# One PSUM tile in place of four pools: denominators between numerators, three rotating halves at the start, paired banks in the drain, w and u loaded first

## The chip, the cores and the metric

The kernel runs on one core of one Trainium2 chip. The metric is device time in microseconds (us) of one execution. Engines are named as in the profile: PE (matmul), DVE (vector), ACT (activation), POOL (GpSimd), SP. Each engine runs its instructions in the order in which the program lists them and waits on semaphores for the others.

## The reference

For each of 16 batches and 256 channels it is a recurrence over 2048 steps (RWKV's "wkv"): a weighted mean of all v so far, the weights being exponentials that decay with w, with a bonus u for the current step.

```python
for t in range(seq_len):
    ww = u + k[b, t]
    qq = np.maximum(pp, ww)
    e1, e2 = np.exp(pp - qq), np.exp(ww - qq)
    output[b, t] = (e1 * aa + e2 * v[b, t]) / (e1 * bb + e2 + 1e-08)
    ww = pp - w + k[b, t]
    qq = np.maximum(ww, k[b, t])
    e1, e2 = np.exp(ww - qq), np.exp(k[b, t] - qq)
    aa, bb, pp = e1 * aa + e2 * v[b, t], e1 * bb + e2, qq
```

k and v are float32 [16, 2048, 256] (33.5 MB each), w and u are [256], and the output has the shape of v.

## The kernel before

The recurrence is cut into chunks of 128 time steps. The 128 partitions hold the 128 steps of a chunk, and a **tile** holds one chunk of four batches: 128 x 1024 values. There are 16 chunks of 4 tiles, so 64 tiles, numbered n = 4c + p. One tile is 512 KB of k, 512 KB of v and 512 KB of output.

A tile passes through these functions:

- `load`: two DMAs, k (tile `kr`) and v (tile `vr`; for every fourth tile from 9 on the DMA casts v itself to bf16, tile `vb`). Nearly all loads and all stores are issued by POOL, in program order, six tiles ahead (`AHEAD`).
- `round_k` (DVE): casts k to the matmul's float32 form, tile `km`, two buffers.
- `logs` (PE): four one- or two-row matmuls (L171) put in the terms of w and u, four full matmuls (L175) add a weighted k. Result: logarithms `X`, two kinds (decayed keys, and keys with the bonus) of two banks each, so four of PSUM's eight banks, one buffer.
- `exps` (ACT): one activation over all four banks, 2048 values a partition, into two planes of the ring `EZR` (12 tiles deep, bf16).
- `cast_v`, `times_v` (DVE): v to bf16, and its product with both planes into the ring's other two planes.
- `den` (PE): running sums along time by triangular matrices, 4 matmuls into `den` (two banks). `recip` (ACT): an Ln and an Exp of 1024 values each give the reciprocal `rd`.
- `num` (PE): the same for one half i of the numerator, 2 matmuls into `num` (one bank). `mult` (DVE): that half times `rd`, 512 values, into `ot`; then `store` (POOL).

Ten iterations (`LAG`) after its `exps`, a tile gets `den` and `recip`; one iteration later `num`, `mult` and `store`. The lag is there for the state that passes from chunk to chunk: some ten small instructions a chunk (`sums`, `copy_sums`, `turn`, `state_logs`, `state_offsets`, `state_weights`, `state_chain`, `turn_back`, `inject`) are spread by the table `later` over six iterations. Their PSUM scratch is the eighth bank (`misc`), and `inject` ends with four small DMAs on SP that write the state into the ring, where `den` and `num` of the next chunk read it.

One loop of 76 iterations does all this; every call is wrapped in `K(...)`, which keeps the written order on each engine. Iterations 0 to 10 write no output yet, and the last 12 (the **drain**) load and exponentiate nothing. In iteration n, `qp = n - 11` is the tile whose numerators are made and `q = n - 10` the tile of `recip`; `den` runs one iteration ahead (`q1`):

```python
num(qp, 0); exps(n); round_k(n + 2); mult(qp, 0); cast_v(n + 1)
num(qp, 1); mult(qp, 1); store(qp); times_v(n); logs(n + 1)
recip(q); den(q1)
```

Of the kernel before, what the change touches and what calls it, by code (L numbers as in the profile page):

```python
# [15 lines left out]
def kernel(  # L16
# [32 lines left out]
    psx = ctx.enter_context(tc.tile_pool(name="psx", bufs=1, space=bass.MemoryType.PSUM))  # L49
    psd = ctx.enter_context(tc.tile_pool(name="psd", bufs=1, space=bass.MemoryType.PSUM))  # L50
    psn = ctx.enter_context(tc.tile_pool(name="psn", bufs=1, space=bass.MemoryType.PSUM))
    psm = ctx.enter_context(tc.tile_pool(name="psm", bufs=1, space=bass.MemoryType.PSUM))
# [30 lines left out]
    K(DVE.memset(I1, 0.0))  # L83
    load(0, SP, SC)
    for r, x in ((0, w), (1, u)):
        for g in range(4):
            K((SP if r == 0 else SC).dma_start(out=wuf[32 * g + r:32 * g + r + 1, :, :], in_=bass.AP(
                tensor=x.tensor, offset=x.offset, ap=[[0, 1], [0, 2], list(x.ap[0])])))
# [76 lines left out]
    def logs(n):  # L165
        X = psx.tile([128, 2, 2, D], F32, tag="X", name="X")
        km = KM[n].rearrange("p (i n) d -> p i (n d)", i=2)
        for q in range(2):
            for i in range(2):
                g = 32 * (2 * q + i)  # L170
                K(PE.matmul(X[:, q, i, :], CO[g:g + 1 + q, :], WU[g:g + 1 + q, :], start=True, stop=False,  # L171
                            tile_position=(g, 0), skip_group_check=True))
        for q, m in enumerate((NLE, NLZ)):
            for i in range(2):
                K(PE.matmul(X[:, q, i, :], m, km[:, i, :], start=False, stop=True, skip_group_check=True))  # L175
        X_of[n] = X

    def exps(n):
        K(SC.activation(ez(n)[:, 0:2], X_of.pop(n), ACT.Exp))  # L179
# [115 lines left out]
    DEN, RD, NUM, OT = {}, {}, {}, {}  # L295

    def den(n):
        d = psd.tile([128, 2, D], F32, tag="den", name="den")
        for m, q in (("L", 0), ("Id", 1)):
            for i in range(2):  # L300
                K(PE.matmul(d[:, i, :], mats[m], ez(n)[:, q, i, :], start=q == 0, stop=q == 1,  # L301
                            skip_group_check=True))
        DEN[n] = d

    def recip(n):
        rd = rpool.tile([128, 2, D], F32, tag="rd", name="rd")
        K(SC.activation(rd, DEN.pop(n), ACT.Ln, scale=RS))  # L307
# [3 lines left out]
    def num(n, i):  # L311
        d = psn.tile([128, D], F32, tag="num", name="num")
        for m, q in (("LN", 2), ("IdN", 3)):
            K(PE.matmul(d, mats[m], ez(n)[:, q, i, :], start=q == 2, stop=q == 3, skip_group_check=True))  # L314
        NUM[n, i] = d

    def mult(n, i):
        if i == 0:
# [2 lines left out]
        K(DVE.tensor_mul(o[:, i, :], NUM.pop((n, i)), RD[n][:, i, :]))  # L321
# [94 lines left out]
```

## Time and profile before

| | |
|---|---|
| median of 3 runs | 387.83 us (386.51 to 391.67) |
| the profiled execution | 386.96 us, span 385.2 us, 1.76 us around it |
| mean granted PE clock | 0.968 |
| busy share of the span | PE 72%, DVE 73%, ACT 67%, POOL 39% |
| HBM | 67.13 MB read, 33.55 MB written |

"Idle before, releaser" is time in which an engine sat idle ahead of an instruction, with what ended it. `[1.65 <-DVE ot L321]` after a row says that the engine had been idle for 1.65 us and that DVE's instruction of line 321 released it. DMA share is the mean busy share of 16 DMA engines; packets of several queues overlap, so it can exceed 1.

### The profile page before, as it was taken

To read this page: it belongs to the slowest core of one execution; us is meant where nothing else is said; L and a number is where in the kernel's file an instruction comes from. 1 tells how busy PE (TensorE), PEld (TensorE's weight loads), DVE (VectorE), ACT (ScalarE), POOL (GpSimd) and SP (SyncE) were. 2 spreads that over 40 slices of the span, in tenths; PEclk is the share of its full clock that TensorE was granted. 3 is DMA by queue.
4 is the path that set the end of the run, shared out by engine and by line. 5 is a ranking of instruction groups with operands and counts; after the bars stand their busy time and mean duration, and the time that the engine had idled before them with its cause. 6 is when DMAs were issued, how large, how long until landed. Compare 5 with 4: busy or idle time off the path is not lost.

```text
span 385.2 us, 4891 instructions
## 1 busy us (share of the span) xinstructions
PE 276.5 (72%) x1664; PEld 135.7 (35%) x1664; DVE 281.5 (73%) x573; ACT 256.9 (67%) x225; POOL 150.7 (39%) x206
## 2 busy tenths in 40 slices
PE   0355868787878787787778787777777977866661
PEld 0123534343433343343324343433333433422220
DVE  1276676969787878889697969787878788765442
ACT  1133345967687777777787877787887677756571
POOL 8144432244244444444445454343444411111221
PEclk9999999988998999999999999999999899989897
DMA  7987995589899999989999999999999962234434
GB/s 248 348 276 199 327 294 167 114 278 282 279 304 266 322 286 300 302 289 283 305 280 316 296 308 285 311 280 311 303 293 302 297 208 92 94 122 155 167 109 163
DMA packets 37688, 97.85 MB, mean 254 GB/s; under 512 B 6160, under 2 KB 15392, under 8 KB 37664
## 3 DMA queue, kind: packets, MB, share of 16 engines
q0 software_dynamic: 32448, 94.91, 78.8%
q1 hardware_dynamic: 4144, 1.59, 1.7%
q10 hardware_dynamic: 1072, 1.06, 0.9%
q8 instruction: 13, 0.21, 0.2%
q14 instruction: 11, 0.09, 0.1%
HBM read 67.13 MB, written 33.55 MB: 261 GB/s over the span
## 4 chain that ended last, share of the span: by engine, by line
PE 28%; DVE 26%; issue 23%; ACT 12%; DMA 5%; POOL 4%; POOLq 0%; DVEq 0%
PE X L175 13%; ACT EZR L179 12%; DVE ot L321 10%; PE num L314 7%; DVE EZR L197 6%; PE X L171 5%; DMA kr<-in_k_dram 4%; POOL out_dram L326 4%; DVE km L162 3%; PE den L301 2%; DMA vr<-in_v_dram 1%; DVE A L249 1%; DVE A L250 1%; DVE CB L270 1%; PE TS L235 1%
## 5 line engine op out<-in xcount | busy, mean ns | idle before, releaser
L179 ACT ACTIVATE EZR<-X 128x2048 bf16<-128x2048 f32 x64 | 120.1, 1877 | 100.5 <-PE X L175 100.5
L321 DVE TENSOR_TENSOR ot<-num,rd 128x512 f32<-128x512 f32 x128 | 88.2, 689 | 63.0 <-PE num L314 28.5
L326 POOL DMA_DIRECT2D out_dram<-ot x64 | 48.5, 758 | 191.7 <-DVE ot L321 189.2
L314 PE MATMUL num<-EZR,LN 128*128 128x512 bf16 x128 | 49.0, 383 | 66.4 <-DVE ot L321 66.4
L197 DVE TENSOR_TENSOR EZR<-EZR,vb 128x2048 bf16<-128x2048 bf16 x64 | 77.9, 1217 | 4.1 <-ACT EZR L179 4.1
L307 ACT ACTIVATE rd<-den 128x1024 f32<-128x1024 f32 x64 | 65.4, 1022 | 14.2 <-PE den L301 13.2
L308 ACT ACTIVATE rd<-rd 128x1024 f32<-128x1024 f32 x64 | 67.7, 1058 | 2.0
L66 POOL DMA_DIRECT2D kr<-in_k_dram x62 | 52.7, 851 | 21.7 <-DVE km L162 18.4
L171 PE MATMUL X<-WU,CO 1*128 1x512 f32 (+1 forms) x256 | 35.4, 543 | 28.4 <-ACT EZR L179 15.2
L175 PE MATMUL X<-km,NLE 128*128 128x512 f32 x128 | 53.1, 500 | 2.3 <-DVE km L162 2.3
L162 DVE CAST km<-kr 128x1024 fp32r<-128x1024 f32 x64 | 44.4, 695 | 12.8 <-PE X L175 7.7
L314 PE MATMUL num<-EZR,IdN 128*128 128x512 bf16 x128 | 49.1, 384 | 0.0
L175 PE MATMUL X<-km,NLZ 128*128 128x512 f32 x128 | 46.1, 445 | 0.0
L314 PEld LDWEIGHTS <-IdN 128*128 128x128 bf16 x128 | 12.5, 97 | 90.8 <-issue 84.2
L301 PE MATMUL den<-EZR,L 128*128 128x512 bf16 x128 | 40.7, 401 | 2.8 <-DMA EZR<-cb 2.4
L301 PE MATMUL den<-EZR,Id 128*128 128x512 bf16 x128 | 39.6, 393 | 0.0
L74 POOL DMA_DIRECT2D vr<-in_v_dram x48 | 36.2, 755 | 0.8 <-DVE vb L192 0.8
L192 DVE CAST vb<-vr 128x1024 bf16<-128x1024 f32 x50 | 34.8, 695 | 0.0
L171 PEld LDWEIGHTS X<-WU,CO 1*128 1x128 f32 (+1 forms) x256 | 13.3, 198 | 56.6 <-ACT EZR L179 21.7
L175 PEld LDWEIGHTS X<-km,NLZ 128*128 128x128 f32 x128 | 27.9, 218 | 7.1
L175 PEld LDWEIGHTS X<-km,NLE 128*128 128x128 f32 x128 | 21.5, 211 | 20.0 <-issue 16.3
L220 PE MATMUL tot<-EZR,OH 128*32 128x256 bf16 x512 | 20.3, 310 | 0.0
(55 smaller groups left out, 170.2 us busy)
## 6 DMA issues: line engine op xcount, KB each, us to landing
out_dram<-ot POOLq DMA_DIRECT2D x64, 512.0 KB, 4.8
kr<-in_k_dram POOLq DMA_DIRECT2D x62, 512.0 KB, 6.9
...
EZR<-cb SPq DMA_DIRECT2D x64, 8.0 KB, 4.6
wuf<-in_w_dram SPq DMA_DIRECT2D x4, 2.0 KB
```

The source lines that it names most:

```text
L66: K((kq or POOL).dma_start(out=kr, in_=src[0]))
L162: K(DVE.tensor_copy(km, kr_of.pop(n)))
L171: K(PE.matmul(X[:, q, i, :], CO[g:g + 1 + q, :], WU[g:g + 1 + q, :], start=True, stop=False, tile_position=(g, 0), skip_group_check=True))
L175: K(PE.matmul(X[:, q, i, :], m, km[:, i, :], start=False, stop=True, skip_group_check=True))
L179: K(SC.activation(ez(n)[:, 0:2], X_of.pop(n), ACT.Exp))
L197: K(DVE.tensor_mul(ez(n)[:, 2:4], ez(n)[:, 0:2], vb.unsqueeze(1).broadcast_to([128, 2, 2, D])))
L301: K(PE.matmul(d[:, i, :], mats[m], ez(n)[:, q, i, :], start=q == 0, stop=q == 1, skip_group_check=True))
L307: K(SC.activation(rd, DEN.pop(n), ACT.Ln, scale=RS))
L308: K(SC.activation(rd, rd, ACT.Exp, scale=-1.0))
L314: K(PE.matmul(d, mats[m], ez(n)[:, q, i, :], start=q == 2, stop=q == 3, skip_group_check=True))
L321: K(DVE.tensor_mul(o[:, i, :], NUM.pop((n, i)), RD[n][:, i, :]))
L326: K(POOL.dma_start(out=out[4 * p:4 * p + 4, c * TC:(c + 1) * TC, :].rearrange("n t d -> t n d"), in_=OT.pop(n)))
```

## The change

Four edits, made together.

**PSUM.** The four pools become one tile `PS` of eight banks, addressed by hand: banks 0 to 3 for the logarithms, 4 and 5 for `den`, 6 for `num`, 7 for the scratch.

**The loop.** `den(q)` moves from the end of the iteration before to a place between `num(qp, 0)` and `num(qp, 1)` of the same iteration as its `recip(q)`. `mult(qp, 0)` moves ahead of `round_k`, `turn_back` right behind `den`, and `cast_v` behind `times_v`.

**The start.** For tiles 0 to 8 (`TURNS`) `logs` and `exps` work by halves of two banks. The halves rotate through three pairs, 0-1, 2-3 and 4-5, since no denominators are made yet. From tile 9 on, the four banks are one buffer again, with one activation.

**The drain.** From iteration 65 on, both numerator halves go into a pair of the now idle logarithm banks, alternating between 0-1 and 2-3, and one DVE instruction of 1024 values multiplies them.

**The loads.** w and u are loaded first, in one DMA each (4 partitions) in place of four, ahead of tile 0 on SP and ACT; the clearing of `wuf` moves from DVE to POOL; tile 1 is loaded by POOL instead of SP and ACT.

```diff
-    K(DVE.memset(wuf, 0.0))
+    K(POOL.memset(wuf, 0.0))
...
+    for r, x, eng in ((0, w, SP), (1, u, SC)):
+        K(eng.dma_start(out=wuf.rearrange("(g r) n d -> r g n d", r=32)[r], in_=bass.AP(
+            tensor=x.tensor, offset=x.offset, ap=[[0, 4], [0, 2], list(x.ap[0])])))
     load(0, SP, SC)
-    for r, x in ((0, w), (1, u)):
-        for g in range(4):
-            K((SP if r == 0 else SC).dma_start(out=wuf[32 * g + r:32 * g + r + 1, :, :], in_=bass.AP(
...
-    load(1, SP, SC)
...
+    PS = ps.tile([128, 8, D], F32, tag="PS", name="PS")
+    DENB, NUMB, MISC = PS[:, 4:6, :], PS[:, 6, :], PS[:, 7, :]
+    TURNS = 9
+
+    def half(n, z):
+        j = (2 * n + z) % 3 if n < TURNS else z
+        return PS[:, 2 * j:2 * j + 2, :]
...
+        if n < TURNS:
+            for q in range(2):
+                rows(q)
+                steps(q)
+        else:
+            rows(0)
+            rows(1)
+            steps(0)
+            steps(1)
 
     def exps(n):
-        K(SC.activation(ez(n)[:, 0:2], X_of.pop(n), ACT.Exp))
+        if n < TURNS:
+            for q in range(2):
+                K(SC.activation(ez(n)[:, q], half(n, q), ACT.Exp))
+        else:
+            K(SC.activation(ez(n)[:, 0:2], PS[:, 0:4, :].rearrange("p (q i) x -> p q i x", q=2), ACT.Exp))
...
-        if out_qp:
-            num(qp, 0)
+        drain = n > NP
+        if drain and out_qp:
+
+            H = PS[:, 2 * (n % 2):2 * (n % 2) + 2, :]
+            for i in range(2):
+                num(qp, H[:, i, :], i)
+        elif out_qp:
+            num(qp, NUMB, 0)
+        if out_q:
+            den(q)
+        small_work(n, "nums")
         if live:
             exps(n)
         small_work(n, "act")
+        if out_q:
+            recip(q)
+        if drain and out_qp:
+            mult(qp, H, slice(0, 2))
+            store(qp)
+        elif out_qp:
+            mult(qp, NUMB, 0)
+        small_work(n, "mid")
         if n + 2 < NP:
             round_k(n + 2)
-        if out_qp:
-            mult(qp, 0)
-        small_work(n, "nums")
-        small_work(n, "mid")
-        if n + 1 < NP:
-            cast_v(n + 1)
-        if out_qp:
-            num(qp, 1)
-            mult(qp, 1)
+        if out_qp and not drain:
+            num(qp, NUMB, 1)
+            mult(qp, NUMB, 1)
             store(qp)
         if live:
             times_v(n)
+        if n + 1 < NP:
+            cast_v(n + 1)
+            logs(n + 1)
...
-        if n + 1 < NP:
-            logs(n + 1)
         small_work(n, "pe")
-        if out_q:
-            recip(q)
-        if out_q1:
-            den(q1)
         small_work(n, "last")
```

Three places show how the order moves. First, ACT at the program's start, with the loads that it issues; before:

```order
L54 ACT_TABLE_LOAD
L74 DMA vr<-in_v_dram 128x4x256
L87 DMA wuf<-in_u_dram 1x2x256 x4
L74 DMA vr<-in_v_dram 128x4x256
L179 ACTIVATE EZR<-X 128x2x1024 x7
```

and with the change:

```order
L51 ACT_TABLE_LOAD
L82 DMA wuf<-in_u_dram 4x2x256
L71 DMA vr<-in_v_dram 128x4x256
L195 ACTIVATE EZR<-PS 128x1024 x14
L258 ACTIVATE LL<-PS 128x2x64
```

u goes ahead of the first v, the second v has left ACT's queue, and the first seven tiles' exponentials are 14 halves. (SP is alike, with w and k.)

Second, PE in one iteration of the middle, from one `logs` to the next; before (L314 is `num`, L301 `den`, L171 and L175 `logs`):

```order
L175 MATMUL X<-km,NLZ 128x512 x2
...
L301 LDWEIGHTS L
L301 MATMUL den<-EZR,L 128x512
...
L301 LDWEIGHTS Id
L301 MATMUL den<-EZR,Id 128x512
L314 LDWEIGHTS LN
L314 MATMUL num<-EZR,LN 128x512
L314 LDWEIGHTS IdN
L314 MATMUL num<-EZR,IdN 128x512
...
L171 MATMUL X<-WU,CO 128x512 x4
```

and with the change (L329 is `num`, L318 `den`, L174 and L179 `logs`):

```order
L179 MATMUL PS<-km,NLZ 128x512 x2
L329 LDWEIGHTS LN
L329 MATMUL PS<-EZR,LN 128x512
L329 LDWEIGHTS IdN
L329 MATMUL PS<-EZR,IdN 128x512
L318 LDWEIGHTS L
L318 MATMUL PS<-EZR,L 128x512
...
L318 LDWEIGHTS Id
L318 MATMUL PS<-EZR,Id 128x512
...
L174 MATMUL PS<-WU,CO 128x512 x4
```

Before, the two `num` blocks stand side by side behind `den`. Now the first `num` comes first, `den` follows, and the second `num` (left out above, the same four rows again) stands between `den` and the next `logs`.

Third, DVE in an iteration of the middle; before (L162 `round_k`, L321 `mult`, L192 `cast_v`, L197 `times_v`):

```order
L162 CAST km<-kr 128x1024
L321 TENSOR_TENSOR ot<-num,rd 128x512
L192 CAST vb<-vr 128x1024
L321 TENSOR_TENSOR ot<-num,rd 128x512
L197 TENSOR_TENSOR EZR<-EZR,vb 128x2x1024
```

and with the change (L165 `round_k`, L335 `mult`, L210 `cast_v`, L215 `times_v`):

```order
L335 TENSOR_TENSOR ot<-PS,rd 128x512
L165 CAST km<-kr 128x1024
L335 TENSOR_TENSOR ot<-PS,rd 128x512
L215 TENSOR_TENSOR EZR<-EZR,vb 128x2x1024
L210 CAST vb<-vr 128x1024
```

The first `mult` is ahead of `round_k`, which now stands between the two, and `cast_v` has moved behind `times_v`.

More of the change, by code (lines that the diff above doesn't have):

```diff
@@ L48 @@
     tiny = ctx.enter_context(tc.tile_pool(name="tiny", bufs=1))
[L49 to L52, printed above, removed]
+    ps = ctx.enter_context(tc.tile_pool(name="ps", bufs=1, space=bass.MemoryType.PSUM))
     K(SC.preload_act_table_set("natural_log_exp_and_others"))
@@ L110 @@
         select(COf, NE, 1.0, -32 * g - 1, 1, [[0, 128]])
-    load(2)
-    load(3)
+    for n in range(1, AHEAD):
+        load(n)
     NLE, NLZ, CO = matrix("NLE", F32R), matrix("NLZ", F32R), matrix("CO", F32R)
@@ L122 @@
     K(DVE.tensor_copy(CO, COf))
-    for n in range(4, AHEAD):
-        load(n)
     mats = {}
@@ L154 @@
     EZR = consts.tile([128, 4, RING, 2, D], BF16, tag="EZR", name="EZR")
-    KM, X_of = {}, {}
+    KM = {}
+    PS = ps.tile([128, 8, D], F32, tag="PS", name="PS")
[4 more added lines that the diff above has]
+        return PS[:, 2 * j:2 * j + 2, :]
     def ez(n):
@@ L165, in logs, with rows, steps @@
     def logs(n):
-        X = psx.tile([128, 2, 2, D], F32, tag="X", name="X")
         km = KM[n].rearrange("p (i n) d -> p i (n d)", i=2)
-        for q in range(2):
+        def rows(q):
             for i in range(2):
                 g = 32 * (2 * q + i)
-                K(PE.matmul(X[:, q, i, :], CO[g:g + 1 + q, :], WU[g:g + 1 + q, :], start=True, stop=False,
+                K(PE.matmul(half(n, q)[:, i, :], CO[g:g + 1 + q, :], WU[g:g + 1 + q, :], start=True, stop=False,
                             tile_position=(g, 0), skip_group_check=True))
-        for q, m in enumerate((NLE, NLZ)):
+        def steps(q):
             for i in range(2):
-                K(PE.matmul(X[:, q, i, :], m, km[:, i, :], start=False, stop=True, skip_group_check=True))
-        X_of[n] = X
-    def exps(n):
-        K(SC.activation(ez(n)[:, 0:2], X_of.pop(n), ACT.Exp))
+                K(PE.matmul(half(n, q)[:, i, :], (NLE, NLZ)[q], km[:, i, :], start=False, stop=True,
+                            skip_group_check=True))
+        if n < TURNS:
[7 more added lines that the diff above has]
+            steps(1)
+    def exps(n):
+        if n < TURNS:
[3 more added lines that the diff above has]
+            K(SC.activation(ez(n)[:, 0:2], PS[:, 0:4, :].rearrange("p (q i) x -> p q i x", q=2), ACT.Exp))
     def cast_v(n):
@@ L213, in sums @@
     def sums(c):
-        t = psm.tile([128, Dm], F32, tag="misc", name="tot")
+        t = MISC[:, 0:Dm]
         for p in range(4):
@@ L231, in turn @@
     def turn(c):
-        TS = psm.tile([128, 6, 2, 2, 8], F32, tag="misc", name="TS")
+        TS = MISC[:, 0:192].rearrange("p (a n e m) -> p a n e m", a=6, n=2, e=2)
         ts = st.pop((c, "ts"))
@@ L276, in turn_back @@
     def turn_back(c):
-        t = psm.tile([128, 128], F32, tag="misc", name="CT")
+        t = MISC[:, 0:128]
         for b in range(4):
@@ L292, in inject, with num, mult @@
                     in_=cb[x:x + 32, :]))
-    DEN, RD, NUM, OT = {}, {}, {}, {}
+    RD, OT = {}, {}
     def den(n):
-        d = psd.tile([128, 2, D], F32, tag="den", name="den")
         for m, q in (("L", 0), ("Id", 1)):
             for i in range(2):
-                K(PE.matmul(d[:, i, :], mats[m], ez(n)[:, q, i, :], start=q == 0, stop=q == 1,
+                K(PE.matmul(DENB[:, i, :], mats[m], ez(n)[:, q, i, :], start=q == 0, stop=q == 1,
                             skip_group_check=True))
-        DEN[n] = d
     def recip(n):
         rd = rpool.tile([128, 2, D], F32, tag="rd", name="rd")
-        K(SC.activation(rd, DEN.pop(n), ACT.Ln, scale=RS))
+        K(SC.activation(rd, DENB, ACT.Ln, scale=RS))
         K(SC.activation(rd, rd, ACT.Exp, scale=-1.0))
         RD[n] = rd
-    def num(n, i):
-        d = psn.tile([128, D], F32, tag="num", name="num")
+    def num(n, bank, i):
         for m, q in (("LN", 2), ("IdN", 3)):
[L314 to L318, printed above, removed]
+            K(PE.matmul(bank, mats[m], ez(n)[:, q, i, :], start=q == 2, stop=q == 3, skip_group_check=True))
+    def mult(n, bank, i):
+        if n not in OT:
             OT[n] = opool.tile([128, 4, Dm], F32, tag="ot", name="ot")
-        o = OT[n].rearrange("p (i n) d -> p i (n d)", i=2)
-        K(DVE.tensor_mul(o[:, i, :], NUM.pop((n, i)), RD[n][:, i, :]))
+        o, rd = OT[n].rearrange("p (i n) d -> p i (n d)", i=2), RD[n]
+        K(DVE.tensor_mul(o[:, i, :], bank, rd[:, i, :]))
     def store(n):
@@ L347 @@
     for n in range(NP + LAG + 2):
-        q1, q, qp = n + 1 - LAG, n - LAG, n - LAG - 1
-        live, out_q1, out_q, out_qp = n < NP, 0 <= q1 < NP, 0 <= q < NP, 0 <= qp < NP
+        q, qp = n - LAG, n - LAG - 1
+        live, out_q, out_qp = n < NP, 0 <= q < NP, 0 <= qp < NP
         if n + AHEAD < NP:
             load(n + AHEAD)
-        if out_qp:
-            num(qp, 0)
+        drain = n > NP
[8 more added lines that the diff above has]
+        small_work(n, "nums")
         if live:
```

1 line of the change is left out of this document (removed).

## The prediction

> **What bounds the kernel now.** I read the slices of the page first, to cut the span into stages, then the chain that ended last in each, then one iteration of the middle in the timeline.
>
> ```profile
> DMA  7987995589899999989999999999999962234434
> ```
>
> No engine is busy for more than 73% of the span (the table above), but the DMA row (40 slices of 9.6 us) shows three stages: a ragged start, a long middle at 9 tenths, and a drain from slice 33 on with little DMA. I treat them apart. The borders are the `exps` of tile 10, the first iteration with `recip`, and that of the last tile, 63:
>
> ```profile
> 15.76 1.88 ACT L179 ACTIVATE EZR<-X 128x2048 bf16<-128x2048 f32 x1 [13.67 <-PE X L175]
> ...
> 64.83 1.88 ACT L179 ACTIVATE EZR<-X 128x2048 bf16<-128x2048 f32 x1 [1.82 <-PE X L175]
> ...
> 336.32 1.88 ACT L179 ACTIVATE EZR<-X 128x2048 bf16<-128x2048 f32 x1 [0.65 <-PE X L175]
> ```
>
> So the start takes 64.8 us, the middle 336.32 - 64.83 = 271.5 us for 53 iterations, 5.12 each, and the drain 385.2 - 336.3 = 48.9 us. In each, another chain ends last.
>
> *Start.* The chain is strictly serial:
>
> ```profile
> 22.95 1.89 ACT EZR L179
> 24.88 0.80 PE X L171 x3
> 25.68 2.02 PE X L175 x4
> 27.72 1.89 ACT EZR L179
> ```
>
> `X` has one buffer, so PE waits for ACT and ACT for PE: 1.89 + 0.80 + 2.02 + 0.06 between = 4.77 us a tile. Ahead of that, tile 0 waits for u and tile 1 for its k:
>
> ```profile
> 0.84 5.64 DMA vr<-in_v_dram
> ...
> 1.50 2.64 SPq L87 DMA_DIRECT2D wuf<-in_w_dram  x4
> 12.30 0.43 DVE L121 CAST WU<-wuf 128x512 fp32r<-128x512 f32 x1 [9.25 <-DMA wuf<-in_u_dram]
> 20.09 1.30 DVE L162 CAST km<-kr 128x1024 fp32r<-128x1024 f32 x2 [5.09 <-DMA kr<-in_k_dram]
> ```
>
> *Middle.* One iteration, seen on three engines:
>
> ```profile
> 213.31 0.61 PE L301 MATMUL den<-EZR,L 128*128 128x512 bf16 x2
> 213.50 1.88 ACT L179 ACTIVATE EZR<-X 128x2048 bf16<-128x2048 f32 x1 [0.65 <-PE X L175]
> 214.18 0.38 PE L314 MATMUL num<-EZR,LN 128*128 128x512 bf16 x1
> 215.69 0.68 DVE L321 TENSOR_TENSOR ot<-num,rd 128x512 f32<-128x512 f32 x1
> 216.43 0.38 PE L314 MATMUL num<-EZR,LN 128*128 128x512 bf16 x1 [1.65 <-DVE ot L321]
> 216.95 0.51 PE L171 MATMUL X<-WU,CO 1*128 1x512 f32 x4
> 218.62 1.88 ACT L179 ACTIVATE EZR<-X 128x2048 bf16<-128x2048 f32 x1 [0.98 <-PE X L175]
> ```
>
> `X` is free at 213.50 + 1.88 = 215.38, but PE begins the next `logs` at 216.95, 1.57 us late. It stands behind the second `num`, which waits for the first `mult` to free the one bank, and that `mult` stands behind `round_k` on DVE. ACT then idles 0.98 us.
>
> **The change, part by part.**
>
> *Start: loads.* w and u now precede everything on SP and ACT, and the first real transfers are issued later by the clearing on POOL, whose price no row shows: at least nothing, at most about 1 us (twice DVE's 0.48), and I take DVE's. With that and one issue in front (2.64 / 4 = 0.66 us), k of tile 0 goes out at about 2.2 instead of 0.8 us, an estimate. By the 5.64 us of the first v it lands at 7.8. `round_k` (0.65) and a first half of `logs` (half of 2.02 plus some delay) lead to the first `exps` at about 10, not 15.8. Tile 1 follows POOL's queue in order, so its 5.1 us wait goes.
>
> *Start: halves.* With three pairs of banks PE fills one pair while ACT reads another, so a tile costs the longest of four: PE 0.80 + 2.02 = 2.82, ACT two halves, DVE `round_k` 0.65, `cast_v` 0.70 and `times_v` 1.22 = 2.6, or the loads. The half activation has no row: between half of 1.88, 0.94, and the whole 1.88; I take the 1.02 of the nearest row, the Ln of 1024 values (L307, below), so 2.04. Then DVE's groups, and the loads:
>
> ```profile
> L197 DVE TENSOR_TENSOR EZR<-EZR,vb 128x2048 bf16<-128x2048 bf16 x64 | 77.9, 1217 | 4.1 <-ACT EZR L179 4.1
> ...
> L192 DVE CAST vb<-vr 128x1024 bf16<-128x1024 f32 x50 | 34.8, 695 | 0.0
> ```
>
> ```profile
> 8.00:26.00 18.00, 6.80 (x21) 3.61 (x22) 8.08 (x16) 3.75 (x2) 5.07 (x7) 1.00 1.04 348
> 160.00:165.00 5.00, 4.54 (x48) 2.32 (x48) 2.94 (x6) 3.71 (x3) 2.48 (x3) 1.00 0.97 336
> 220.00:300.00 80.00, 61.84 (x409) 31.04 (x410) 66.81 (x132) 62.35 (x56) 36.46 (x47) 0.99 0.96 299
> ```
>
> (Columns: window, length, busy us of PE, PEld, DVE, ACT and POOL, granted clock, DMA share, GB/s.) While loads alone were queued, 348 GB/s moved: 1.05 MB a tile in 3.0 us. That is the longest of the four. `exps` of tile 10 starts at 10 + 10 x 3.0 = **40 us** instead of 64.8: **-24.8 us**.
>
> *Middle: den between the numerators.* Behind `logs`, PE now does the first `num` and `den` while ACT runs `exps`; the first `mult` leads DVE's iteration, so the second `num` can pass before `exps` ends. The 1.57 us are gone. What is late next is the question. Per iteration the third window gives DVE 66.81 / 80 x 5.12 = 4.28 us, ACT 3.99, PE 3.96, none changed by the edit (`round_k` covers the PE's second `num`). With small stalls I take 4.4 for DVE. But the loads and stores of an iteration are 299 GB/s x 5.12 us = 1.53 MB, and their share, 0.96, is near the 1.04 of the saturated start: 0.96 x 5.12 / 1.04 = 4.73 us. At 336 GB/s, the best of the 5 us windows that I read in the middle, it is 4.55; at share 1.00 it is 4.92. I take **4.7** for 53 iterations, 249.1 us: **-22.4 us**. The tail without loads would go faster and the first iterations with few stores too; I leave both in the 4.7.
>
> The new order adds a wait: `recip(q)` follows `den` of its own iteration. Queued behind it on ACT is the next `exps`. `den` takes 214.18 - 213.31 = 0.87 and the `num` ahead of it about half that, 1.3 together, which the 1.88 of `exps` hides. If DVE's second `mult`, which frees the bank for that `num`, comes so late that `exps` is over, the cover is gone and ACT waits up to 1.3 us.
>
> *Drain.* Both halves go into idle banks, so the ping-pong of `num` and `mult` ends.
>
> ```profile
> L321 DVE TENSOR_TENSOR ot<-num,rd 128x512 f32<-128x512 f32 x128 | 88.2, 689 | 63.0 <-PE num L314 28.5
> ...
> L307 ACT ACTIVATE rd<-den 128x1024 f32<-128x1024 f32 x64 | 65.4, 1022 | 14.2 <-PE den L301 13.2
> L308 ACT ACTIVATE rd<-rd 128x1024 f32<-128x1024 f32 x64 | 67.7, 1058 | 2.0
> ...
> 358.32 0.28 DVE L285 CAST cb<-CT 128x128 bf16<-128x128 f32 x1
> 365.71 1.02 ACT L307 ACTIVATE rd<-den 128x1024 f32<-128x1024 f32 x1 [3.65 <-PE den L301]
> 368.86 1.02 ACT L307 ACTIVATE rd<-den 128x1024 f32<-128x1024 f32 x1 [1.03 <-PE den L301]
> 371.66 1.02 ACT L307 ACTIVATE rd<-den 128x1024 f32<-128x1024 f32 x1 [0.69 <-PE den L301]
> 379.21 0.69 DVE L321 TENSOR_TENSOR ot<-num,rd 128x512 f32<-128x512 f32 x1 [0.68 <-PE num L314]
> ```
>
> The last four tiles wait for the state, whose DMAs, and a `den` on an idle PE behind them, let the first Ln start 365.71 - 358.32 = 7.4 us after the cast `cb`; that stays. Behind it a tile took 371.66 - 368.86 = 2.80 us and now takes ACT's 1.02 + 1.06 = 2.1, if `den` of the next tile runs under the Exp. From `cb` on: 7.4, four tiles of 2.1, one wide `mult` (between 0.69 and 1.38, I take 1.3 with its delay), and the 385.2 - 379.9 = 5.3 us of store behind the last `mult`: 22.4 us, against 385.2 - 358.3 = 26.9. Ahead of `cb` lie five iterations in 22.0 us, paced by the small steps of the state, each of which waits for another engine; the wide `mult` saves 2 x 0.69 - 1.2 = 0.2 us in each, so 1.0. Sum **-5.5 us**, a drain of 43.4 (bounds: nothing, if the small steps set the pace throughout, and 12 x 0.7 = 8.4).
>
> *Sum.* Span 385.2 - 24.8 - 22.4 - 5.5 = 332.5, plus the 1.76 around it: **334 us**. The profiled execution (386.96) lies 0.9 under the median of the three runs shown, which changes nothing here.
>
> [...] The start moved 348 GB/s at share 1.04, the best mixed window 336. [...]
>
> **The rivals.**
>
> 1. *DVE sets the middle, not DMA.* For it: the middle's DMA share was never held at a plateau by demand, and single windows move more than the mean. Against: 336 was the most that a 5 us window showed. At 4.4 us: 40 + 233.2 + 43.4 + 1.8 = 318 us.
> 2. *The middle stays at 5.12*, since ACT's wait for `logs` turns into one for `den`, or the mixed DMA stream is full already at 0.96. For it: the share itself. Against: the start's 1.04. 40 + 271.4 + 43.4 + 1.8 = 357 us.
> 3. *The start gains half:* loads starve or PE is cold. The L175 matmuls of a tile took 2.02 us in the start, and later
>
> ```profile
> 207.64 1.13 PE X L175 x4
> ```
>
> At 4.5 a tile in place of 3.0, 40 becomes 55 and the result 349 us. Against: even the cold 2.82 is under 3.0.
> 4. *Slower: the throttle.* Where PE was packed, the granted clock fell:
>
> ```profile
> 76.00:80.00 4.00, 4.00 (x42) 2.22 (x40) 2.59 (x3) 2.11 (x2) 2.32 (x3) 0.62 0.98 337
> ```
>
> PE's 3.96 us fill 77% of an iteration now and 84% at 4.7. If that kept the clock down, the pace would be 3.96 / clock; below a clock of 0.68 (5.86 us) the kernel is slower by 2%, and at 0.62 it takes 6.39: 40 + 338.7 + 45.2 = 424 us. Against: the middle's mean is 0.99. [...]
>
> 5. *It doesn't do what it says:* waits are kept for the whole tile `PS`, so halves never overlap. Then an iteration is `exps`, PE, Ln and two `mult` in a row, 1.88 + 3.96 + 1.02 + 1.38 = 8.2 us, over 500 us in all. Against: `EZR` is one tile too, and PE reads it while DVE and ACT write other slots.
>
> **Chances.** Forecast 0.54 (own range 326 to 345, from 4.55 to 4.9 a tile), first rival 0.15, second 0.18, third 0.07, fourth 0.04, fifth 0.02. Range 318 to 357: it reaches to both neighbours' values and leaves out the halves beyond them, with the last two, some 0.2. A measurement here tells about 2% from no change: under 380 faster, over 395.6 slower. The first three rivals and the forecast are all under 380; some of the fourth is in between: faster 0.93, same 0.03, slower 0.04.
>
> **What would show it.** After: tile 0's `exps` near 10 us and the next ones 3.0 apart, with DMA share at 1.0 in the first 40 us; in the middle no wait of `num` for `mult` over 1 us, the pace at 4.7, DMA share at 1.0 or more, and waits for k (`round_k <- DMA kr`) that before had none after 20 us; about 320 GB/s. If those waits don't appear and the pace is 4.4, rival 1 holds; if ACT waits for `den` at 5.1, rival 2. In the drain, ACT without idle time for the last four tiles, 2.1 apart, and the last `exps` 43 us before the end. The forecast fails if mixed DMA traffic has less reserve than the pure loads, or if `den` is not done when `exps` ends.

## The result and the profile after

| | before | changed |
|---|---|---|
| median | 387.17 us (385.67 to 391.67, 4 runs) | 346.8 us (343.3 to 348.8, 4 runs) |
| ratio, 95% interval | | 0.894 [0.885, 0.903] |
| the profiled execution, its span | 386.96, 385.2 us | 347.02, 345.3 us |
| busy share of the span: PE, DVE, ACT, POOL | 72, 73, 67, 39% | 83, 80, 75, 47% |

The kernel is some 40 us faster. The time is 13 us above the forecast of 334: just outside the forecast's own range (326 to 345), inside the whole one (318 to 357). The same borders as before cut the span (ACT in the timeline of the changed kernel: start, length, line, operation, idle time before it and what ended that):

```profile
9.88 1.02 ACT L195 ACTIVATE EZR<-PS 128x1024 bf16<-128x1024 f32 x1 [7.79 <-PE PS L179]
...
52.76 1.88 ACT L197 ACTIVATE EZR<-PS 128x2048 bf16<-128x2048 f32 x1 [2.90 <-PE PS L179]
...
302.94 1.86 ACT L197 ACTIVATE EZR<-PS 128x2048 bf16<-128x2048 f32 x1
```

| stage | before | forecast | measured |
|---|---|---|---|
| start, to the `exps` of tile 10 | 64.8 | 40 | 52.8 |
| middle, 53 iterations | 271.5 (5.12 each) | 249.1 (4.70) | 250.2 (4.72) |
| drain | 48.9 | 43.4 | 42.4 |

The start alone holds the difference to the forecast, 12.8 us.

*Start.* PE, and one window (its columns as in the prediction):

```profile
8.62 1.22 PE L179 MATMUL PS<-km,NLE 128*128 128x512 f32 x2 [3.33 <-DVE km L165]
9.77 0.79 PE L174 MATMUL PS<-WU,CO 2*128 2x512 f32 x2
10.49 1.22 PE L179 MATMUL PS<-km,NLZ 128*128 128x512 f32 x2
11.64 0.79 PE L174 MATMUL PS<-WU,CO 1*128 1x512 f32 x2
...
8.00:26.00 18.00, 17.38 (x37) 7.57 (x38) 13.30 (x27) 9.21 (x9) 12.46 (x18) 1.00 1.03 350
```

PE never pauses: a pair of row matmuls (L174) and a pair of steps (L179) per half, 11.64 - 9.77 = 1.87 us, so 3.75 us a tile. Two row matmuls take 0.79 us; before, all four of a tile took 0.80, so they had run side by side. The halves, which the change issues as rows, steps, rows, steps, split them into two groups, and each costs the whole time.

*Middle.* One chunk of the state is four iterations (ACT's `exps`, and every other row that waited):

```profile
111.84 1.86 ACT L197 ACTIVATE EZR<-PS 128x2048 bf16<-128x2048 f32 x1
114.05 0.36 ACT L275 ACTIVATE G<-A 128x192 f32<-128x192 f32 x1 [0.35 <-DVE A L271]
116.86 1.88 ACT L197 ACTIVATE EZR<-PS 128x2048 bf16<-128x2048 f32 x1 [0.44 <-PE PS L179]
121.97 1.88 ACT L197 ACTIVATE EZR<-PS 128x2048 bf16<-128x2048 f32 x1 [1.22 <-PE PS L179]
124.36 1.03 ACT L323 ACTIVATE rd<-PS 128x1024 f32<-128x1024 f32 x1 [0.51 <-PE PS L318]
126.48 1.88 ACT L197 ACTIVATE EZR<-PS 128x2048 bf16<-128x2048 f32 x1
130.44 1.86 ACT L197 ACTIVATE EZR<-PS 128x2048 bf16<-128x2048 f32 x1
```

The `exps` are 5.02, 5.11, 4.51 and 3.96 us apart, and so in chunk after chunk (medians over the chunks: 5.03, 5.10, 4.52, 3.96; before 5.12, 5.09, 5.38, 4.70). The change took 0.86 and 0.74 us from the third and the fourth iteration and next to nothing from the first two. The last is now ACT's own work, 1.88 + 1.02 + 1.06. In the first two ACT still waits for `logs`, for this reason (DVE and PE in a first iteration, here one with 5.9 us):

```profile
207.37 0.19 DVE L271 TENSOR_SCALAR A<-A 128x64 f32<-128x64 f32 x1
207.47 0.68 DVE L335 TENSOR_TENSOR ot<-PS,rd 128x512 f32<-128x512 f32 x1
...
208.20 0.38 PE L329 MATMUL PS<-EZR,LN 128*128 128x512 bf16 x1 [1.65 <-DVE ot L335]
...
208.73 0.51 PE L174 MATMUL PS<-WU,CO 1*128 1x512 f32 x4
209.16 1.22 PE L179 MATMUL PS<-km,NLE 128*128 128x512 f32 x2
```

DVE's first `mult` (207.47) follows directly on the last of the seven steps of `state_offsets`, the second `num` waits 1.65 us for it, and `logs` stand behind that `num`. Such a wait, 1.63 to 1.86 us, comes once in each of 13 chunks. The iteration shown has a further loss: behind the wait PE runs its steps at 1.22 us a pair instead of 0.73, with a granted clock of 0.59 (208.7 to 211.0 us). In the second iteration `state_chain` stands ahead of the first `mult`, and `turn_back` on PE waits for it too (0.71 us at 118.85). The third iteration's 0.51 us is another wait: `recip` waits for `den`, because `sums` (1.06 us at 121.86) stands ahead of it on PE. From tile 10 to tile 63 ACT waits 21.2 us for `logs` in the first and second iterations, 4.4 us for `state_offsets` itself in the first (L275, the 0.35 above) and 9.8 us for `den` in the third. The groups of the whole span:

```profile
L197 ACT ACTIVATE EZR<-PS 128x2048 bf16<-128x2048 f32 x55 | 102.9, 1872 | 27.1 <-PE PS L179 26.7
...
L329 PE MATMUL PS<-EZR,LN 128*128 128x512 bf16 x128 | 50.2, 393 | 28.6 <-DVE ot L335 28.5
...
L165 DVE CAST km<-kr 128x1024 fp32r<-128x1024 f32 x64 | 44.6, 696 | 8.4 <-DMA kr<-in_k_dram 6.4
```

ACT's wait for the whole `logs` fell from 100.5 to 26.7 us (the halves of the start wait another 24.4), PE's for `mult` from 66.4 to 28.5. The waits for k, 6.4 us, all lie in the start.

*Drain:*

```profile
327.81 0.59 PE L318 MATMUL PS<-EZR,L 128*128 128x512 bf16 x2 [3.37 <-DMA EZR<-cb]
...
328.96 1.02 ACT L323 ACTIVATE rd<-PS 128x1024 f32<-128x1024 f32 x1 [3.24 <-PE PS L318]
...
332.28 1.02 ACT L323 ACTIVATE rd<-PS 128x1024 f32<-128x1024 f32 x1 [1.20 <-PE PS L318]
...
334.41 1.02 ACT L323 ACTIVATE rd<-PS 128x1024 f32<-128x1024 f32 x1
...
338.69 1.22 DVE L335 TENSOR_TENSOR ot<-PS,rd 128x1024 f32<-128x1024 f32 x1 [0.91 <-ACT rd L324]
```

The first of the last four tiles waits for the state, the second comes 3.32 us later, and the other two follow at ACT's 2.13 us.

### The profile page after: what moved, and what is told of

It reads as the page before. It is cut to its first block, busy times and chain, and to the rows that moved or that the text cites. A ratio compares the mean times of both kernels' runs of the same rounds, so it can differ in the third digit from the quotient of the medians.

```text
span 345.3 us, 4824 instructions
## 1 busy us (share of the span) xinstructions
PE 285.6 (83%) x1664; PEld 137.9 (40%) x1664; DVE 277.7 (80%) x562; ACT 258.6 (75%) x234; POOL 162.9 (47%) x209
## 3 DMA queue, kind: packets, MB, share of 16 engines
q1 hardware_dynamic: 3612, 1.06, 1.4%
## 4 chain that ended last, share of the span: by engine, by line
PE 40%; DVE 26%; issue 18%; DMA 7%; POOL 4%; ACT 2%; SPq 1%; POOLq 0%
PE PS L179 13%; PE PS L329 10%; DVE EZR L215 8%; DVE ot L335 6%; PE PS L318 6%; PE PS L174 6%; DMA EZR<-cb 5%; POOL out_dram L340 4%; DVE vb L210 4%; PE PS L238 4%; DMA kr<-in_k_dram 2%; DVE CB L288 1%; PE PS L253 1%; DVE A L267 1%; DVE A L268 1%
## 5 line engine op out<-in xcount | busy, mean ns | idle before, releaser
L197 ACT ACTIVATE EZR<-PS 128x2048 bf16<-128x2048 f32 x55 | 102.9, 1872 | 27.1 <-PE PS L179 26.7
L335 DVE TENSOR_TENSOR ot<-PS,rd 128x512 f32<-128x512 f32 (+1 forms) x118 | 86.4, 733 | 38.4 <-issue 11.1
L323 ACT ACTIVATE rd<-PS 128x1024 f32<-128x1024 f32 x64 | 65.3, 1021 | 21.0 <-PE PS L318 20.6
L215 DVE TENSOR_TENSOR EZR<-EZR,vb 128x2048 bf16<-128x2048 bf16 x64 | 77.9, 1217 | 2.2 <-ACT EZR L197 1.1
L329 PE MATMUL PS<-EZR,LN 128*128 128x512 bf16 x128 | 50.2, 393 | 28.6 <-DVE ot L335 28.5
L179 PE MATMUL PS<-km,NLE 128*128 128x512 f32 x128 | 53.9, 507 | 3.3 <-DVE km L165 3.3
L165 DVE CAST km<-kr 128x1024 fp32r<-128x1024 f32 x64 | 44.6, 696 | 8.4 <-DMA kr<-in_k_dram 6.4
L329 PE MATMUL PS<-EZR,IdN 128*128 128x512 bf16 x128 | 49.7, 388 | 0.0
L179 PE MATMUL PS<-km,NLZ 128*128 128x512 f32 x128 | 48.2, 462 | 0.0
L174 PE MATMUL PS<-WU,CO 1*128 1x512 f32 (+1 forms) x256 | 42.6, 546 | 5.1 <-DVE CO L117 4.5
L71 POOL DMA_DIRECT2D vr<-in_v_dram x49 | 42.5, 867 | 6.4 <-DMA vr<-in_v_dram 3.8
L318 PE MATMUL PS<-EZR,L 128*128 128x512 bf16 x128 | 39.7, 393 | 5.4 <-DMA EZR<-cb 4.3
L318 PE MATMUL PS<-EZR,Id 128*128 128x512 bf16 x128 | 38.9, 386 | 0.0
L195 ACT ACTIVATE EZR<-PS 128x1024 bf16<-128x1024 f32 x18 | 18.4, 1023 | 24.4 <-PE PS L179 24.4
L210 DVE CAST vb<-vr 128x1024 bf16<-128x1024 f32 x50 | 34.7, 695 | 0.0
L174 PEld LDWEIGHTS PS<-WU,CO 1*128 1x128 f32 (+1 forms) x256 | 15.8, 198 | 39.0 <-issue 25.5
L179 PEld LDWEIGHTS PS<-km,NLZ 128*128 128x128 f32 x128 | 26.8, 218 | 9.6 <-issue 3.9
L179 PEld LDWEIGHTS PS<-km,NLE 128*128 128x128 f32 x128 | 21.8, 213 | 21.2 <-issue 14.9
L329 PEld LDWEIGHTS <-IdN 128*128 128x128 bf16 x128 | 12.7, 99 | 43.1 <-issue 41.2
```

Source lines behind the costliest of these rows:

```text
L174: K(PE.matmul(half(n, q)[:, i, :], CO[g:g + 1 + q, :], WU[g:g + 1 + q, :], start=True, stop=False, tile_position=(g, 0), skip_group_check= ...
L179: K(PE.matmul(half(n, q)[:, i, :], (NLE, NLZ)[q], km[:, i, :], start=False, stop=True, skip_group_check=True))
L197: K(SC.activation(ez(n)[:, 0:2], PS[:, 0:4, :].rearrange("p (q i) x -> p q i x", q=2), ACT.Exp))
L210: K(DVE.tensor_copy(vb, vr))
L215: K(DVE.tensor_mul(ez(n)[:, 2:4], ez(n)[:, 0:2], vb.unsqueeze(1).broadcast_to([128, 2, 2, D])))
L318: K(PE.matmul(DENB[:, i, :], mats[m], ez(n)[:, q, i, :], start=q == 0, stop=q == 1, skip_group_check=True))
```

## The experiments

Every kernel is the changed one with the edit shown; line numbers shift by a few where lines were added. Ratios are to the kernel before on the same chip.

### What sets the start: the row matmuls

`e1_rows4`: also for the first nine tiles

```diff
-            for q in range(2):
-                rows(q)
-                steps(q)
+            rows(0)
+            rows(1)
+            steps(0)
+            steps(1)
```

> Only the start changes: the four row matmuls of a tile (w and u) stand together ahead of the four full ones, on the same three rotating pairs. Theory (PE sets the start: in the changed kernel two rows take 0.79 us, as long as four before, so a tile costs 2 x (0.72 + 1.15) = 3.75 us of PE): a tile then costs 0.72 + 2 x 1.15 = 3.0 us, the exps of tile 8 start some 6 us earlier, and the run takes about 341 us against 347. Rival (loads set the start): the pace stays at 3.7 and the time at 347.

Measured: 344.4 us, ratio 0.891 [0.882, 0.900]. On PE:

```profile
10.00:15.00 5.00, 5.00 (x15) 1.00 1.03 351
...
11.04 1.22 PE L179 MATMUL PS<-km,NLE 128*128 128x512 f32 x2
...
13.05 1.12 PE L174 MATMUL PS<-WU,CO 1*128 1x512 f32 x4
14.10 1.22 PE L179 MATMUL PS<-km,NLE 128*128 128x512 f32 x2
```

(In the window's row the columns behind the length are PE's busy time, granted clock, DMA share, GB/s.) The `exps` of tiles 0 to 5 come 14.10 - 11.04 = 3.06 us apart, and tile 5's at 24.54 us instead of 28.61. That the split of the row matmuls set the pace is shown. The gain is 4.1 us at tile 5 and 5.4 at tile 8 (37.12 for 42.48), near the 6 expected. Tile 9 gives 1.0 of it back, and tile 10 comes at 48.4 us. These 4.3 us are too few for the two intervals to tell the kernels apart.

`e9_no_turns`: no halves in the start, all else as changed

```diff
-    TURNS = 9
+    TURNS = 0
```

> Only edit: no three halves in the start; the logs of every tile go to the same four banks and one Exp reads them, as they do from tile 9 on. Theory H (halves in turn are what lets TensorE run through in the start): logs and exps take turns again, 2.8 us of matmuls and 1.9 us of Exp, 4.77 us a tile as before, from a first exps at 11 us: tile 10 at 59 to 62 us instead of 52.8, the time 7 to 9 us longer than the changed kernel (about 355 us). Rival L (the start is earlier only because its loads are): tile 10 stays at about 53 us and the time at 347 us.

Measured: 349.9 us, ratio 0.908 [0.898, 0.917].

```profile
9.98 1.88 ACT L197 ACTIVATE EZR<-PS 128x2048 bf16<-128x2048 f32 x1 [7.89 <-PE PS L179]
14.75 1.88 ACT L197 ACTIVATE EZR<-PS 128x2048 bf16<-128x2048 f32 x1 [2.89 <-PE PS L179]
...
56.54 1.88 ACT L197 ACTIVATE EZR<-PS 128x2048 bf16<-128x2048 f32 x1 [1.73 <-PE PS L179]
```

The 4.77 us a tile are back, as theory H has it, but tile 10 is only 3.8 us later than with halves. So of the 12.1 us that the start gained, 64.83 - 56.54 = 8.3 come from the loads and the rest of the change, and 3.8 from the halves, for which the prediction had counted ten times 4.77 - 3.0, 17.7 us. (With the row matmuls together, as in `e1_rows4`, the halves are worth 56.54 - 48.42 = 8.1.) The time lies between the two theories, and its interval overlaps that of the changed kernel.

### PE's slow pace

`e8_warm`: work for PE ahead of the first `logs`

```diff
+    for _ in range(16):
+        K(PE.matmul(NUMB, WB[:, 0:128], WB, start=True, stop=True, skip_group_check=True))
     logs(0)
```

> Only edit: 16 bf16 matmuls of 128x512 on a constant tile, issued on TensorE ahead of the first logs (their result goes to the numerator bank and is not used). Theory W (TensorE stays at its slow pace of 1.22 us for a pair of L179 until dense bf16 work has run for some us): the logs of the start run at 0.73 us a pair, and the exps of tiles 1 to 8 come as fast as the loads at 348 GB/s let them, 3.0 us apart: tile 10 at about 43 to 45 us, the time about 338 us. Rival: the slow pace belongs to these matmuls in the start, or comes back at once; pairs stay at 1.22 us, tile 10 at 53 us, 347 us, or later if the 16 matmuls, at 0.43 us each, hold the first logs up beyond 8.6 us.

Measured: 346.3 us, ratio 0.887 [0.874, 0.901].

```profile
1.53 5.15 PE L360 MATMUL PS<-WB 128*128 128x512 bf16 x16 [1.53 <-DVE WB L80]
...
7.95 0.73 PE L181 MATMUL PS<-km,NLE 128*128 128x512 f32 x2 [0.85 <-DVE km L167]
...
14.66 1.05 PE L181 MATMUL PS<-km,NLZ 128*128 128x512 f32 x2
```

Both theories have a part. The bf16 matmuls do bring PE to its fast pace, 0.73 us a pair. The `logs` don't hold it, with 2.0 us of waits for k among them: 8 us behind the last bf16 matmul a pair takes 1.05, and up to 44 us all take 1.05 or 1.22 us again. Tile 10 comes at 48.3 us.

`e10_held`: the four rows together, the 16 matmuls, and 5 more behind the `logs` of each of the first tiles

```diff
+        if n < 9:
+            for _ in range(5):
+                K(PE.matmul(NUMB, WB[:, 0:128], WB, start=True, stop=True, skip_group_check=True))
```

> Three edits in the start alone: the four row matmuls of a tile together, 16 unused bf16 matmuls ahead of the first logs, and 5 more behind the logs of each of the first ten tiles, which shall hold TensorE at its fast pace. Theory W: a pair of L179 stays at 0.73 us throughout; the exps of the start come 3.0 to 3.1 us apart until the state's steps of chunk 0, tile 10 at 41 to 44 us instead of 52.8, and the same middle: 335 to 338 us. Rival: the matmuls of the logs fall back to 1.22 us a pair in spite of them, and the unused matmuls then cost 5 x 0.43 = 2.1 us a tile: tile 10 at 60 us, 355 us.

Measured: 344.2 us, ratio 0.889 [0.875, 0.903]. PE keeps 0.73 us a pair through most of the start, as theory W has it, yet tile 10's `exps` is at 48.0 us, not 41 to 44. PE now waits for others:

```profile
29.14 0.73 PE L181 MATMUL PS<-km,NLE 128*128 128x512 f32 x2 [1.69 <-DVE km L167]
...
40.77 0.40 PE L300 MATMUL PS<-Id,CB 128*128 128x128 bf16 x4 [3.50 <-DVE x L294]
```

The first is tile 6, for its k; the second is `turn_back` of chunk 0, which waits for `state_chain` and has the next `logs` behind it. DVE is the full engine here: from 28 to 40 us it is busy for 11.81 of 12 us, with the state's steps beside `round_k`, `cast_v` and `times_v`. So in this order of the program a faster PE alone doesn't bring the 40 us of the forecast.

### What sets the middle: DMA or the state

`e2_less_dma`: the v of tiles 16 on isn't loaded, except where the DMA casts it (a constant tile stands in, and v has five buffers in place of six)

```diff
+            if n >= 16:
+                vr_of[n] = vfix
+                return
             vr = vpool.tile([128, 4, Dm], F32, tag="vr", name="vr")
```

> Left out: the loads of v from tile 16 on, except the cast ones of every fourth tile; DVE casts a constant tile instead, so its work is the same. One v buffer fewer, for space. A quarter of the middle's DMA traffic is gone. Theory of the prediction (DMA sets the pace of the middle): the pace falls from 4.7 to DVE's 4.4 or below, and the run to about 331 us. Rival (the state's DVE steps ahead of the first mult hold up the second num and with it logs): the pattern of 3.96, 5.0, 5.1, 4.5 us stays, the pace 4.65 to 4.7, the time 345 to 347.

Measured: 347.4 us in one run. The window 100 to 220 us of the changed kernel, then of this one:

```profile
100.00:220.00 120.00, 103.92 (x688) 52.11 (x689) 107.84 (x217) 102.00 (x90) 63.95 (x77) 0.97 1.02 325
```

```profile
100.00:220.00 120.00, 102.39 (x670) 50.83 (x684) 106.65 (x216) 100.85 (x90) 46.41 (x56) 0.97 0.84 237
```

A quarter less traffic (237 instead of 325 GB/s), and the same intervals, 5.02, 5.08, 4.53, 3.96, at 4.72 us in the mean. DMA doesn't set the middle.

`e3_no_state`: the state between chunks is left out whole

```diff
-    for c in range(NST):
+    for c in range(0):
```

> Left out: the whole state (sums to inject), so the output lacks what earlier chunks add. All loads, stores and the large instructions stay. Rival (the state's DVE steps set the pace above 4.0): the middle runs at ACT's 1.88 + 1.02 + 1.06 = 3.96 to 4.0 us, about 308 us in all. Theory of the prediction (DMA): the pace can't fall under 1.53 MB by some 336 GB/s, 4.55 us; about 335 us.

Measured: 289.6 us in one run. From tile 10 to 63 it takes 255.11 - 47.66 = 207.5 us, 3.91 an iteration:

```profile
L197 ACT ACTIVATE EZR<-PS 128x2048 bf16<-128x2048 f32 x55 | 103.0, 1872 | 7.8 <-PE PS L179 6.2
...
100.00:220.00 120.00, 104.30 (x480) 47.76 (x488) 110.81 (x145) 116.90 (x92) 73.54 (x91) 1.00 1.06 382
```

ACT is busy 97% of that window and hardly waits. The state costs 0.8 us an iteration; which part of it, this run doesn't say, since its work on PE, ACT and DVE is left out together. (The time is below the rival's 308 because the start, 47.7 us, and the drain, 32.8, are shorter too.) Mixed loads and stores reach 382 GB/s here, at a DMA share of 1.06; the changed kernel moved 325 at 1.02. So a share near 1 was no limit.

`e4_old_middle`: the new start and drain, but the loop of the middle in the order of before

```diff
+        if not drain:
+            if out_qp:
+                num(qp, NUMB, 0)
+            if live:
+                exps(n)
...
+            if out_q:
+                recip(q)
+            if 0 <= n + 1 - LAG < NP and n < NP:
+                den(n + 1 - LAG)
+            small_work(n, "last")
+            continue
```

> Start, loads and drain as changed, but iterations up to 64 in the old order (den at the end of the iteration before, round_k ahead of the first mult, cast_v ahead of the second). By the traces the middle goes back from 250.2 to about 271 us: 347 + 21 = 368 us. If the new PSUM tile or the earlier start were the cause of the gain in the middle, it would stay near 347.

Measured: 369.7 us, ratio 0.956 [0.949, 0.962]. The middle takes 326.52 - 52.06 = 274.5 us, 5.18 an iteration, and the intervals have the medians of before, 5.11, 5.09, 5.38, 4.70. This is what was expected. Between the two ratios lie 0.062, or 24 us: the order alone, with the same loads and the same banks.

### Trying to take the state out of the way

`e5_copy`, the changed kernel again, with no edit:

> The changed kernel itself once more, on the chip of the next three kernels, as the base that they are compared with. Both theories: about 347 us, tile 10's exps at about 52.8 us, 4.72 us a tile after that.

346.2 us, ratio 0.895 [0.885, 0.904].

`e6_logs_first`: on PE the next `logs` ahead of the second `num`

```diff
+        if n + 1 < NP:
+            logs(n + 1)
         if out_qp and not drain:
             num(qp, NUMB, 1)
...
-            logs(n + 1)
```

> Only edit: the logs of the next tile are issued on TensorE ahead of the second numerator instead of behind it. Theory A (the middle is 4.72 us a tile because the state's VectorE steps stand ahead of the first product, the second numerator waits for it, and the logs stand behind that numerator): the logs no longer wait for VectorE, ScalarE's wait for L179 falls from 26.7 us to under 10, and the pace falls towards VectorE's own work of 4.3 to 4.4 us an iteration: 53 x 0.3 = 16 us less, 331 us. Theory B (VectorE's products and the one numerator bank hold TensorE anyway, at the next first numerator): pace 4.6 to 4.7, 343 to 347 us.

Measured: 366.3 us, ratio 0.949 [0.942, 0.956], 20 us slower than the changed kernel; neither theory had that.

```profile
L197 ACT ACTIVATE EZR<-PS 128x2048 bf16<-128x2048 f32 x55 | 102.5, 1864 | 16.3 <-PE PS L179 16.3
L335 DVE TENSOR_TENSOR ot<-PS,rd 128x512 f32<-128x512 f32 (+1 forms) x118 | 86.6, 734 | 60.0 <-PE PS L329 43.6 <-ACT rd L324 10.0 <-issue 2.1
```

ACT's wait does fall, from 26.7 to 16.3 us, but DVE now waits 43.6 us for `num`, mostly the second, a wait that was 5.2 us before the edit. `times_v`, `cast_v` and the state's steps stand behind that product, and DVE has the least to spare (107.84 of 120 us busy in the changed kernel's window above).

`e7_logs_rows4` adds to that edit the one of `e1_rows4`:

> The edit of the kernel before this one, and the four row matmuls of a tile together in the start too (as in the experiment on the rows). Both theories: 4 us less at tile 10 than without the second edit (48.4 instead of 52.8 us), and the same pace: 327 us by theory A, 339 to 343 us by B. If the start's gain is given back later, the same time as without it.

362.0 us, ratio 0.941 [0.931, 0.952], with tile 10 at 46.9 instead of 50.1 us. The start's 3.2 us are gained, but the time misses both theories, with DVE waiting 42.5 us for `num`.

`e11_held_order`: the start of `e10_held`, and in the middle `den`, `num`, `logs`, `num` on PE, with `times_v` and `inject` ahead of the second product on DVE

```diff
-        elif out_qp:
-            num(qp, NUMB, 0)
         if out_q:
             den(q)
-        small_work(n, "nums")
+        if out_qp and not drain:
+            num(qp, NUMB, 0)
...
+        if n + 1 < NP:
+            logs(n + 1)
+        small_work(n, "nums")
+        if live:
+            times_v(n)
+        small_work(n, "late")
         if out_qp and not drain:
             num(qp, NUMB, 1)
             mult(qp, NUMB, 1)
```

> The start of the kernel before this one, and another order of the middle: TensorE does the denominators ahead of the first numerator, the next logs ahead of the second numerator, and VectorE does times_v and inject ahead of the second product. Theory O (putting the logs first cost 20 us because VectorE then waited for the second numerator, 43.6 us in all at L329, with times_v queued behind it): with times_v ahead of that product VectorE has work while the logs run; VectorE's wait for L329 falls under 15 us, the pace to 4.4 us, and the time to 318 to 325 us. Rival: the single numerator bank holds both engines in turn whatever the order; the pace is 4.7 or more, 335 us and up.

Measured: 401.8 us against 388.3 before. No interval of the ratio was formed, but each of its four runs (394.8 to 408.0) is longer than all seven of the kernel before (384.3 to 393.9).

```profile
L321 PE MATMUL PS<-EZR,L 128*128 128x512 bf16 x113 | 40.2, 430 | 47.2 <-DMA EZR<-cb 41.7 <-ACT rd L326 4.0 <-ACT EZR L200 1.2
```

To get `logs` in front, `turn_back` and `inject` had moved behind them, and the state's small DMAs then land after `den` needs them: 41.7 us of waits where the changed kernel has 4.3, and ACT waits 75 us for `den`. DVE's wait for the products is 22.0 us, not the under 15 of theory O, but in an iteration that now waits elsewhere; theory O stays open. Its start is the shortest of all, with tile 10 at 44.8 us: `turn_back` stands behind the `logs` here, and tile 9 follows tile 8 after 2.77 us, where `e10_held` has 5.48.

`e12_pool`: the kernel of `e1_rows4`, and in it the seven steps of `state_offsets`, 1.4 us a chunk on DVE, done by POOL. (The kernel of `e1_rows4` takes 297.26 - 48.42 = 248.8 us from tile 10 to 63, 4.70 a tile.) On POOL they are eleven, right behind `state_logs`; the minimum is written with add, max and subtract

```diff
-        K(DVE.scalar_tensor_tensor(nF, LL[:, 1, 2 * c + 1:2 * c + 3, :], -1.0, LL[:, 1, 2 * c + 2:2 * c + 4, :],
-                                   ALU.mult, ALU.subtract))
+        K(POOL.tensor_add(nF, LL[:, 1, 2 * c + 1:2 * c + 3, :], LL[:, 1, 2 * c + 2:2 * c + 4, :]))
...
-                               (s + 3, "act", state_logs), (s + 3, "last", state_offsets),
+                               (s + 3, "act", state_logs), (s + 3, "act", state_offsets),
```

> [...] Theory A (the middle is 4.7 us a tile because the state's VectorE steps stand ahead of the first product and so of the logs): the tile after the offsets, 5.0 us apart before, comes down to about 4.0, the pace to 4.45, and the time by 53 x 0.25 = 13 us to about 331 us. Rival P (the state costs its time by its TensorE work, the sums, turns and turn_back of about 2.8 us a chunk, or by the waits around it): the tile after the offsets stays at 5.0 us, the pace at 4.7, the time at 344 us. If GpSimd's steps last over 0.3 us each or wait behind DMA issues, ScalarE waits for the offsets at L275 and its neighbours, and the time is over 350 us.

Measured: 364.7 us (358.2 to 367.3), ratio 0.932 [0.923, 0.940], as the third case has it. The profiled execution, the longest of the six:

```profile
L277 ACT ACTIVATE G<-A 128x192 f32<-128x192 f32 x16 | 5.8, 362 | 39.3 <-POOL A L273 39.3
```

The same step, L270, takes 0.28 us in one chunk and 1.83 in another, where DVE's `times_v` and `cast_v` run at that time:

```profile
201.01 1.83 POOL L270 TENSOR_SCALAR d<-d 128x32 f32<-128x32 f32 x1
...
218.94 0.28 POOL L270 TENSOR_SCALAR d<-d 128x32 f32<-128x32 f32 x1
```

```profile
200.95 1.22 DVE L216 TENSOR_TENSOR EZR<-EZR,vb 128x2048 bf16<-128x2048 bf16 x1
202.08 0.70 DVE L211 CAST vb<-vr 128x1024 bf16<-128x1024 f32 x1
```

POOL's step ends with the cast, at 202.84 us for 202.78, and `times_v` starts 0.06 us ahead of it; at the short one DVE's last instruction had ended at 217.54. The 32 steps at L270 take 0.68 us in the mean. What holds the long one back isn't shown. POOL also issues the loads and stores, which stand behind its steps: the store of a product that ended at 201.03 us is issued at 204.49, 0.07 us behind the last step. In two of the 16 chunks ACT didn't have to wait for POOL; in the second of them:

```profile
222.94 1.88 ACT L198 ACTIVATE EZR<-PS 128x2048 bf16<-128x2048 f32 x1 [0.49 <-PE PS L179]
...
226.98 1.86 ACT L198 ACTIVATE EZR<-PS 128x2048 bf16<-128x2048 f32 x1
```

There the first iteration took 4.04 us instead of 5.03 (4.52 in the other). That speaks for theory A, but it follows a stall of 7.6 us in which DVE had caught up, so it is no proof. That the state sets the middle is shown (`e3_no_state`); that it does so by its DVE steps ahead of the first `mult`, more than by its 2.4 us of matmuls a chunk (37.8 us of PE over 16 chunks), is read from the waits of the trace and isn't shown by an experiment. The 9.8 us in the third iterations are on the side of the matmuls.

No version with the whole work beats the changed kernel by more than the intervals.

## Why the prediction was right and wrong

- **The first `exps`**: right, 9.88 us for "about 10". The clearing on POOL took 0.52 us, for which DVE's 0.48 had been taken, the cast of tile 0's k began at 7.87 for 7.8, and the wait for the k of tile 1 is gone.
- **The start's pace**: wrong, and this is the whole miss. The step that failed is "a tile costs the longest of four: PE 0.80 + 2.02 = 2.82", with the loads' 3.0 as the longest and the result multiplied by ten. Three things were in its way:

```profile
28.61 1.02 ACT L195 ACTIVATE EZR<-PS 128x1024 bf16<-128x1024 f32 x1 [0.85 <-PE PS L179]
...
34.18 1.02 ACT L195 ACTIVATE EZR<-PS 128x1024 bf16<-128x1024 f32 x1 [2.68 <-PE PS L179]
...
38.73 1.02 ACT L195 ACTIVATE EZR<-PS 128x1024 bf16<-128x1024 f32 x1 [1.48 <-PE PS L179]
...
47.99 1.88 ACT L197 ACTIVATE EZR<-PS 128x2048 bf16<-128x2048 f32 x1 [2.62 <-PE PS L179]
```

  The PE term is 3.75, because the row matmuls cost 0.79 twice: 10 x 0.75 = 7.5 us. The `sums` and `turn` of chunk 0, which the sum left out of an engine that is full, delay tiles 6 and 7: they come 5.57 and 4.55 us after the tile before, 2.6 more than 2 x 3.75. And tiles 9 and 10 don't turn through the halves at all, since `TURNS` is 9: with `turn_back` of chunk 0 ahead of tile 9 they take 5.51 and 4.77 us, 2.8 more than 2 x 3.75. With the 0.1 us by which tile 0 came early, that is 12.8, the miss. The first part is shown by `e1_rows4`, the other two are read from the trace. The order of the diff (rows, steps, rows, steps) and the number 9 were there to be read. Rival 3 is the one that came: the start gained 12.1 of the 24.8 us, half, and its 349 us is nearer to the 346.8 than the forecast is. It had a chance of 0.07, and its causes, starved loads or a cold PE, were not the main one: the slow pace was in the 2.82 already. The argument against it, "even the cold 2.82 is under 3.0", failed with the same term.
- **The middle**: the number is right (4.72 for 4.7), its cause is wrong, so the number is luck. It had been taken from DMA, "0.96 x 5.12 / 1.04 = 4.73"; `e2_less_dma` refutes that, and the waits for k that it called for didn't come. Two of its signs did, a DMA share at 1.0 or more (1.02) and about 320 GB/s (325), but 1.53 MB in 4.72 us make 324 GB/s whatever sets the pace. The 4.4 us for DVE "with small stalls" were an average over four unlike iterations: two stand near 5.1 because the state's steps delay the first `mult`, one at 4.52 because `sums` delays `den`, one is at ACT's 3.96. So rival 1's reasoning (DVE and not DMA) was nearer, with the wrong pace. The step that failed is "the 1.57 us are gone": in the two iterations with the state's steps they are not, and "no wait of `num` for `mult` over 1 us" is refuted by the 1.65 above. That the order saved 24 us all the same is shown by `e4_old_middle`.
- **The best rates**: a window of `e3_no_state` moved 382 GB/s at share 1.06, above the 348 and 336 of the prediction, and DMA did not bind in the middle (`e2_less_dma`). So neither of the two was the most that the DMA engines can move.
- **The wait of `recip` for `den`**: as stated it is hidden in most iterations. In all 13 third iterations of the middle ACT does wait, mostly 0.51 us, but for `sums` on PE and not for a late second `mult`; the sum had no term for that. ACT's idle time before L323 is 21 us in all, against 14 before.
- **The throttle** (rival 4) did not decide: the mean granted clock is 0.966, before 0.968. In the middle PE did slow down where it fell (0.59 from 208.7 to 211.0 us, with a pair of L179 at 1.22 us for 0.73).
- **The drain**: right in its mechanism, with some luck in the sum. From `cb` (322.76) to the end it is 22.5 us for 22.4, but the first Ln comes 6.2 us behind `cb` for 7.4, and the next one 3.32 behind it for 2.1, since PE's `den` there takes 1.06 and 0.96 us; the two errors cancel. The last two tiles are 2.13 apart for 2.1, the wide product takes 1.22 for 1.2, and ahead of `cb` lie 19.8 us for 21.0.
